# Hybrid attention/mLSTM layer: PSUM banks of the second merge, and the places and emission points of the output weights

## The chip, the cores and the metric

One core of one Trainium2 chip. The metric is the device time of one execution in microseconds (us). Before the change, three runs gave 844.54, 844.98 and 847.42 us, so the median is 844.98 us.

## The reference

One decoder layer works on `x`, 1024 tokens by 1024 features, in float32. A pre-norm and one wide projection feed two mixers, a differential attention `ya` (4 heads) and an mLSTM `yb` (4 heads). What the change touches is the end of the layer:

```
merged = sigmoid(ga) * (ya @ w_a) + sigmoid(gb) * (yb @ w_b)
out    = merged @ w_out
x      = x + rmsnorm(out, norm_post)
```

Here `ya` and `yb` are 1024 x 512, `w_a` and `w_b` 512 x 1024 and `w_out` 1024 x 1024.

## The kernel before

Every float32 matrix product is done as three products of a rounded high part and a low remainder (high x high, and the two mixed ones). `split` (line 113) makes the two parts of a tile: ScalarE (ACT) casts the high part, and VectorE (DVE) subtracts it to get the low part. So each weight tile and each intermediate tile costs one ACT and one DVE instruction before TensorE (PE) can use it.

The layer's last three stages are these.

The first merge (`merge_b`, line 1092) multiplies the mLSTM outputs by `w_b`. It is a generator, and its matmuls are pulled piece by piece between the steps of the last attention heads, so that PE has work while softmax runs on DVE and ACT. `merge` (line 1062) works through 8 column blocks `d` of 128 and two token halves, so 16 blocks of 12 matmuls. Each block accumulates in one PSUM bank, and DVE line 1083 then reads the bank and the stored gate `tg` and writes the product back into `tg`. `keep_b` stores that in DRAM (`m_d`).

The second merge does the same with the attention outputs and `w_a`. Its `finish_a` (line 1151) loads the stored first half (`mb`), adds it on DVE (line 1154) and splits the sum into high and low parts `M[kh, T, e]`: `kh` is the half of the columns, `T` the half of the tokens and `e` the high or low part. All 16 blocks take their bank from `acc`, a pool of 3. The other five banks are in the pool `misc`, used by scores, transposes and half of the output tiles.

The output stage (from line 1191) goes over the column halves `cc` and the eight token tiles `tt`. Each of the 16 groups is 24 matmuls, over `kt` from 0 to 7, with `M` as the stationary and `wide[cc, kh, k, e]`, the split output weights, as the moving operand. The order within a `kt` is M high with weight high, M high with weight low, M low with weight high. `out_weights(cc, kh)` loads one quarter of `w_out` in two pieces `g` of 512 KB through `raw_tile` (4 buffers, shared with the merges' weights and with `load_y`), and splits each piece into tiles called here the homes: for (0, 0) the tiles 21h and 21l, for (0, 1) t2h and t2l, for (1, 0) t1h and t1l, for (1, 1) three `wc` buffers and slot 12. The tiles t1 and t2 hold the attention outputs `ys_a` until the second merge's matmuls end. The tiles 21h and 21l hold two of the mLSTM outputs until the first merge ends. The residual rows `xr` take slots 8 to 11, which the last attention head uses before (slot 8: its output; 9 and 10: keys; 11: the mask).

Each engine runs its instructions in an order that is fixed when the program is built. The planner takes the emission order as priority, but lets a later instruction go ahead where it expects the engine to be free and the operands to be there. So an instruction can run well before the place where its line stands, and then holds up what is queued behind it if its data come later than planned. All transfers shown are issued from one queue, SP, in such an order.

Of the kernel before, what the change touches and what calls it, by code (L numbers as in the profile page):

```python
# [10 lines left out]
F32R = mybir.dt.float32r  # L11
# [5 lines left out]
P = 128  # L17
# [22 lines left out]
def kernel(  # L40
# [16 lines left out]
    nc = tc.nc  # L57

    cp = ctx.enter_context(tc.tile_pool(name="cp", bufs=1))
    hp = ctx.enter_context(tc.tile_pool(name="hp", bufs=1))  # L60
# [8 lines left out]
    w_a_v = w_a[0].rearrange("(k p) n -> p k n", p=P)  # L69
    w_b_v = w_b[0].rearrange("(k p) n -> p k n", p=P)  # L70
    w_out_v = w_out[0].rearrange("(k p) n -> p k n", p=P)
# [7 lines left out]
    def mm(*args, **kw):  # L79
        pin(nc.tensor.matmul(*args, **kw))  # L80
# [7 lines left out]
    def acc(name):  # L88
        return ps_acc.tile([P, 512], F32, tag="acc", name=name)
# [4 lines left out]
    def slot(i, shape, name, dtype=F32):  # L94
        return tp.tile(shape, dtype, tag=f"T{i}", name=name)

    def part(name, dtype=F32):
        return tp.tile([P, 512], dtype, tag="st", name=name, bufs=5)

    def temp(name):  # L100
        return tp.tile([P, 512], F32, tag="tm", name=name, bufs=4)

    def raw_tile(shape, name):
        return wp.tile(shape, F32, tag="raw", name=f"raw_{name}", bufs=4)

    def wc_tile(shape, name, dtype=F32R):
        return wp.tile(shape, dtype, tag="wc", name=name, bufs=3)

    def drain(gen):
        for _ in gen:  # L110
            pass

    def split(raw, hi, lo):
        nc.scalar.copy(hi, raw)  # L114
        nc.vector.tensor_sub(lo, raw, hi.bitcast(F32))
# [370 lines left out]
    def hs_(T):  # L486
        return slice(T * 512, T * 512 + 512)
# [561 lines left out]
        left[0] -= pulled[0] - was  # L1049


    def load_y(slot0, heads, tags):
        ys = []
        for h in heads:
            r = raw_tile([P, S], f"yr{slot0 + h}")
            nc.sync.dma_start(r, y_d[slot0 + h])
            t = hp.tile([P, 2, S], F32R, tag=f"h{tags[h]}", name=f"y{slot0 + h}")
            split(r, t[:, 0], t[:, 1])
            ys.append(t)
        return ys  # L1060

    def merge(name, w_v, which, ys, finish):
        for d in range(8):
            if d % 2 == 0:
                r = raw_tile([P, 4, 2, P], f"{name}{d}")
                nc.sync.dma_start(
                    r.rearrange("p k n c -> p k (n c)"), w_v[:, :, d * P : d * P + 256]
                )
            w = wc_tile([P, 2, 4, P], f"{name}w{d}")
            split(r[:, :, d % 2], w[:, 0], w[:, 1])  # L1070
            for half in range(2):
                tg = temp("tg")
                nc.sync.dma_start(tg, g_d[which * 8 + d][:, hs_(half)])
                ps = acc("mrg")
                for kt in range(4):
                    for j, (a, b) in enumerate(((0, 0), (0, 1), (1, 0))):
                        mm(
                            ps, w[:, a, kt], ys[kt][:, b, hs_(half)],
                            start=(kt == 0 and j == 0), stop=(kt == 3 and j == 2),
                        )  # L1080
                    if kt % 2:
                        yield 1.4
                nc.vector.scalar_tensor_tensor(  # L1083
                    out=tg, in0=tg, scalar=1.0, in1=ps, op0=ALU.add, op1=ALU.mult
                )
                finish(d, half, tg)
# [5 lines left out]
    ys_a = []  # L1092

    def merge_b():
        ys = load_y(4, range(4), ("11h", "11l", "21h", "21l"))
        n = 0
        for due in merge("mb", w_b_v, 1, ys, keep_b):
            yield due
            n += 1
            if n == 20:  # L1100
                ys_a.extend(load_y(0, range(3), YA))
        done.add("mb")


    PAIR, MB = 7 * 12 * 0.2325, 16 * 12 * 0.2325
    fill.append(run_pairs(pairs))
    fill.append(merge_b())
    total = len(pairs) * PAIR + MB
    weave(gate_chain())
# [35 lines left out]
    for kh in range(2):  # L1145
        for T in range(2):
            for e in range(2):
                tag = (("t3h", "t3l"), ("22h", "22l"), ("t4h", "t4l"), ("11h", "11l"))[kh * 2 + T][e]
                M[kh, T, e] = hp.tile([P, 4, 512], F32R, tag=f"h{tag}", name=f"m{kh}{T}{e}")

    def finish_a(d, half, tg):
# [2 lines left out]
        nc.vector.tensor_add(tg, tg, mb)  # L1154
        split(tg, M[d // 4, half, 0][:, d % 4], M[d // 4, half, 1][:, d % 4])

    drain(merge("ma", w_a_v, 0, ys_a, finish_a))


    npost = slot(13, [P, D], "npost")  # L1160
# [1 line left out]
    orow = [slot(i, [P, D], f"o_{i}") for i in range(8)]  # L1162
    ssq = cp.tile([P, NT, 2], F32, name="ssq")

    wide = {}

    def out_weights(cc, kh):

        if (cc, kh) == (1, 1):
            home = [  # L1170
                wc_tile([P, 2, 512], f"wo{n}") if n < 3 else slot(12, [P, 2, 512], "wo3", F32R)
                for n in range(4)
            ]
            for k in range(4):
                for e in range(2):
                    wide[cc, kh, k, e] = home[(k // 2) * 2 + e][:, k % 2]
            dst = [[home[g * 2 + e] for e in range(2)] for g in range(2)]
        else:
            names = (("21h", "21l"), ("t2h", "t2l"), ("t1h", "t1l"))[cc * 2 + kh]
            home = [hp.tile([P, 4, 512], F32R, tag=f"h{n}", name=f"wo{n}") for n in names]  # L1180
            for k in range(4):
                for e in range(2):
                    wide[cc, kh, k, e] = home[e][:, k]
            dst = [[home[e][:, g * 2 : g * 2 + 2] for e in range(2)] for g in range(2)]
        for g in range(2):
            r = raw_tile([P, 2, 512], f"o{cc}{kh}{g}")
            k0 = kh * 4 + g * 2
            nc.sync.dma_start(r, w_out_v[:, k0 : k0 + 2, cc * 512 : cc * 512 + 512])
            split(r, *dst[g])

    for cc in range(2):
        for kh in range(2):
            out_weights(cc, kh)
        c0 = cc * 512
        for tt in range(NT):
            ts_ = slice(tt * P, (tt + 1) * P)
            js = slice((tt % 4) * P, (tt % 4 + 1) * P)
            ps = (misc if tt % 2 else acc)("out")
            for kt in range(KT):
                for i, (a, b) in enumerate(((0, 0), (0, 1), (1, 0))):  # L1200
                    mm(
                        ps, M[kt // 4, tt // 4, a][:, kt % 4, js], wide[cc, kt // 4, kt % 4, b],
                        start=(kt == 0 and i == 0), stop=(kt == KT - 1 and i == 2),
                    )
            junk = part("oj")
            nc.scalar.activation(  # L1206
                junk, ps, AF.Square, scale=D ** -0.5, accum_out=ssq[:, tt, cc : cc + 1]
            )
            orr = orow[tt]
            nc.vector.tensor_mul(orr[:, c0 : c0 + 512], ps, npost[:, c0 : c0 + 512])  # L1210
            if cc == 0:
                nc.gpsimd.tensor_scalar(
                    ssq[:, tt, 0:1], ssq[:, tt, 0:1], 1.0, 4.0 * EPS, ALU.mult, ALU.add
                )
                continue
            st = sp.tile([P, 3], F32, tag="ost", name="ost")
            nc.gpsimd.tensor_add(st[:, 0:1], ssq[:, tt, 0:1], ssq[:, tt, 1:2])
            nc.gpsimd.tensor_tensor(st[:, 2:3], st[:, 0:1], mhalf[:, 0:1], ALU.pow)
            xr = slot(8 + tt % 4, [P, D], "xr")
            nc.sync.dma_start(xr, x[0, ts_, :])  # L1220
            for n0 in range(0, D, 512):
                ns = slice(n0, n0 + 512)
                nc.vector.scalar_tensor_tensor(
                    out=orr[:, ns], in0=orr[:, ns], scalar=st[:, 2:3], in1=xr[:, ns],
                    op0=ALU.mult, op1=ALU.add,
                )
                nc.sync.dma_start(out[0, ts_, ns], orr[:, ns])
# [28 lines left out]
```

## Time and profile before

| what | value |
|---|---|
| median of three runs | 844.98 us |
| the profiled execution | 845.01 us |
| its span | 843.3 us |
| PE busy | 828.1 us (98%) |
| DVE busy | 571.8 us (68%) |
| ACT busy | 401.1 us (48%) |
| POOL busy | 38.4 us (5%) |

The span is the time from the first to the last recorded instruction, and 1.71 us of the profiled execution lie outside it. Matmuls overlap one another, so a recorded matmul is longer than the distance to the next one. A stall is best read from the distance between starts. In a row of the timeline, the part in brackets says how long the engine sat idle before the instruction and what ended that.

### The profile page before, as it was taken

Reading aid. Unit: us, or ns where it says so; the run is one execution under the profiler, and the core shown is the slowest. Engines: PE = TensorE matmul, PEld = TensorE weight load, DVE = VectorE, ACT = ScalarE, POOL = GpSimd, SP = SyncE. Lnnn points to the kernel's source line nnn. Section 1 sums busy time; section 2 is a strip of 40 time slices with the busy share of each in tenths; the row PEclk is TensorE's granted clock in tenths of the full one; section 3 lists DMA queues with packets and bytes.
Section 4 is the critical chain, followed back from the end, with each engine's and each line's share of the span. In section 5 each row is a group of like instructions: output and inputs, shape, how many; then the busy total and the mean of one; then the engine's idle time right before and its main releaser. Section 6 shows DMA issues by size and latency. Waiting matters only on the chain.

```text
span 843.3 us, 12218 instructions
## 1 busy us (share of the span) xinstructions
PE 828.1 (98%) x4282; PEld 705.7 (84%) x4282; DVE 571.8 (68%) x1161; ACT 401.1 (48%) x892; POOL 38.4 (5%) x70
## 2 busy tenths in 40 slices
PE   9999999999999999999999999999999999999997
PEld 7998888888888888888888888878888887778885
DVE  6996969769659766568767865587586645881133
ACT  6654545544554544446646654466676412341110
POOL 1100000000000000020010000000100000000011
PEclk9999999999999999999999999999999999999999
DMA  7712342442552557276256336433766869840062
GB/s 246 213 38 76 94 146 59 134 158 56 170 162 75 175 157 231 84 211 200 69 184 204 126 94 206 150 137 96 226 205 225 284 195 295 274 137 1 1 199 100
DMA packets 100482, 128.44 MB, mean 152 GB/s; under 512 B 8666, under 2 KB 60098, under 8 KB 100420
## 3 DMA queue, kind: packets, MB, share of 16 engines
q1 hardware_dynamic: 100420, 127.66, 48.1%
q8 instruction: 34, 0.56, 0.3%
q14 instruction: 28, 0.23, 0.1%
HBM read 88.27 MB, written 39.35 MB: 151 GB/s over the span
## 4 chain that ended last, share of the span: by engine, by line
PE 84%; DMA 7%; DVE 4%; ACT 2%; issue 2%; SPq 1%; POOL 0%; DVEq 0%; POOLq 0%; ACTq 0%
PE out L80 10%; PE tok L80 6%; PE S L80 4%; PE pv L80 3%; DMA m_d<-tg 3%; PE mrg L80 2%; PE pT L83 2%; PE num L80 1%; DMA zs<-z_d 1%; PE qkb0Y L80 1%; PE g04Y L80 1%; PE g00Y L80 1%; PE za1Y L80 1%; PE g02Y L80 1%; PE g12Y L80 1%
## 5 line engine op out<-in xcount | busy, mean ns | idle before, releaser
L956 ACT ACTIVATE p<-p,ast 128x128 f32<-128x128 f32 (+7 forms) x64 | 49.6, 776 | 29.7 <-DVE ast L955 21.6
L949 DVE CUSTOM_DVE_ANT_0 p<-S,gm 128x384 f32<-128x384 f32 (+5 forms) x96 | 49.9, 554 | 18.2 <-PE S L80 16.5
L1210 DVE TENSOR_TENSOR o<-out,npost 128x512 f32<-128x512 f32 x16 | 11.1, 691 | 57.0 <-ACT oj L1206 57.0
L80 PE MATMUL mrg<-y,maw 128*128 128x512 f32 x192 | 44.0, 390 | 1.8 <-DVE tg L1083 1.8
L80 PE MATMUL mrg<-y,mbw 128*128 128x512 f32 x192 | 44.9, 391 | 0.0
L80 PEld LDWEIGHTS mrg<-y,maw 128*128 128x128 f32 x192 | 36.0, 188 | 9.7 <-DVE tg L1083 2.2
L1206 ACT ACTIVATE oj<-out 128x512 f32<-128x512 f32 x16 | 9.6, 598 | 69.2 <-PE out L80 69.1
L80 PEld LDWEIGHTS mrg<-y,mbw 128*128 128x128 f32 x192 | 35.8, 188 | 7.3
L80 PEld LDWEIGHTS pv<-va,pT 128*128 128x128 f32 x288 | 37.2, 191 | 2.7
L80 PE MATMUL pv<-va,pT 128*128 128x128 f32 x288 | 37.4, 275 | 0.0
L80 PE MATMUL S<-khh,qs 128*128 128x384 f32 (+5 forms) x96 | 34.7, 367 | 0.0
L80 PE MATMUL S<-kll,qs 128*128 128x384 f32 (+5 forms) x96 | 32.4, 342 | 0.4 <-DMA kll<-qk_d 0.4
L1083 DVE SCALAR_TENSOR_TENSOR tg<-tg,mrg 128x512 f32<-128x512 f32 x32 | 21.8, 682 | 16.0 <-PE mrg L80 13.1
L754 DVE SCALAR_TENSOR_TENSOR cv<-pad,cols,cv 128x1024 f32<-128x1024 f32 x24 | 30.7, 1279 | 0.2
L970 DVE SCALAR_TENSOR_TENSOR p<-p,ast,p 128x128 f32<-128x128 f32 (+7 forms) x32 | 26.1, 816 | 0.7
L823 ACT ACTIVATE junk<-raw 128x128 bf16<-128x128 f32 x32 | 9.9, 310 | 32.3 <-DVE raw L818 32.1
L83 PE MATMUL pT<-ident,p 128*128 128x128 f32 x144 | 21.2, 274 | 3.5 <-DVE p L970 3.4
L995 ACT ACTIVATE oa<-pv 128x128 f32<-128x128 f32 x32 | 8.9, 277 | 30.9 <-PE pv L80 30.8
L986 ACT COPY pT<-pT 128x512 f32<-128x512 f32 (+3 forms) x48 | 21.7, 488 | 3.3 <-PE pT L83 3.2
L80 PE MATMUL out<-wo,m 128*128 128x512 f32 x96 | 23.1, 389 | 0.0
L114 ACT CAST m<-tg 128x512 fp32r<-128x512 f32 x16 | 9.9, 621 | 24.4 <-DVE tg L1154 24.4
L80 PEld LDWEIGHTS out<-wo,m 128*128 128x128 f32 x96 | 18.0, 188 | 3.7
(1240 smaller groups left out, 2474.9 us busy)
## 6 DMA issues: line engine op xcount, KB each, us to landing
raw_g<-in_w_in_dram SPq DMA_DIRECT2D x16, 512.0 KB, 4.1
g_d<-g SPq DMA_DIRECT2D x32, 256.0 KB, 3.8
tg<-g_d SPq DMA_DIRECT2D x32, 256.0 KB, 3.8
raw_qkb<-in_w_in_dram SPq DMA_DIRECT2D x16, 256.0 KB, 3.1
z_d<-zt SPq DMA_DIRECT2D x16, 256.0 KB, 3.1
zs<-z_d SPq DMA_DIRECT2D x16, 256.0 KB, 5.2
raw_qka<-in_w_in_dram SPq DMA_DIRECT2D x16, 256.0 KB, 3.1
qk_d<-qah SPq DMA_DIRECT2D x16, 256.0 KB, 2.1
```

Source lines behind the costliest of these rows:

```text
L80: pin(nc.tensor.matmul(*args, **kw))
L83: pin(nc.tensor.transpose(out=out, in_=in_, identity=ident))
L114: nc.scalar.copy(hi, raw)
L754: nc.vector.scalar_tensor_tensor(out=cv, in0=pad[:, t : t + S], scalar=cols[:, t * 8 + blk : t * 8 + blk + 1], in1=cv, op0=ALU.mult, op1=A ...
L823: nc.scalar.activation(junk, raw[:, c, 0:P], AF.Square, accum_out=stbs[h, c // 4][:, 1, c % 4 : c % 4 + 1])
L949: nc.vector.tensor_tensor_reduce(out=pr[:, n0:n1], in0=pss[:, : n1 - n0], in1=gm[:, (7 - i) * P + n0 : (7 - i) * P + n1], scale=-0.125, sc ...
L956: nc.scalar.activation(pr[:, :nk], pr[:, :nk], AF.Exp, bias=nm, scale=-1.0, accum_out=sth[:, c, i : i + 1],)
L970: nc.vector.scalar_tensor_tensor(out=p0[:, :nk], in0=p1[:, :nk], scalar=st[:, 3:4], in1=p0[:, :nk], op0=ALU.mult, op1=ALU.add,)
L986: nc.scalar.copy(pT[:, j0:j1], pt[:, 0 : (j1 - j0) * P].rearrange("p (j t) -> p j t", t=P))
L1083: nc.vector.scalar_tensor_tensor(out=tg, in0=tg, scalar=1.0, in1=ps, op0=ALU.add, op1=ALU.mult)
L1206: nc.scalar.activation(junk, ps, AF.Square, scale=D ** -0.5, accum_out=ssq[:, tt, cc : cc + 1])
L1210: nc.vector.tensor_mul(orr[:, c0 : c0 + 512], ps, npost[:, c0 : c0 + 512])
```

## The change

The second merge takes its banks in turn from `acc` and `misc`. The first quarter of the output weights, (0, 0), gets the tiles t4h and t4l as homes, and its two pieces are emitted inside the first merge, after its 8th and its 14th yield of 32. The second quarter, (0, 1), gets slots 8 to 11. The quarters (1, 0) and (1, 1) get t2 and t1. `M[1, 0]` moves from t4h and t4l to 21h and 21l. The quarters other than (0, 0) are emitted where they were. The `wc` buffers and slot 12 no longer hold output weights.

```diff
+    def out_weights(cc, kh, g):
+        if (cc, kh) not in homes:
+            tags = {(0, 0): ("t4h", "t4l"), (1, 0): ("t2h", "t2l"), (1, 1): ("t1h", "t1l")}
+            if (cc, kh) in tags:
+                two = [
+                    hp.tile([P, 4, 512], F32R, tag=f"h{t}", name=f"wo{t}") for t in tags[cc, kh]
+                ]
+                homes[cc, kh] = [[two[e][:, n * 2 : n * 2 + 2] for e in range(2)] for n in range(2)]
+            else:
+                four = [slot(8 + n, [P, 2, 512], f"wo{n}", F32R) for n in range(4)]
+                homes[cc, kh] = [four[0:2], four[2:4]]
...
+        r = raw_tile([P, 2, 512], f"o{cc}{kh}{g}")
+        k0 = kh * 4 + g * 2
+        nc.sync.dma_start(r, w_out_v[:, k0 : k0 + 2, cc * 512 : cc * 512 + 512])
+        split(r, *dst)
...
-    def merge(name, w_v, which, ys, finish):
+    def merge(name, w_v, which, ys, finish, banks=None):
+        banks = banks or (acc,)
...
-                ps = acc("mrg")
+                ps = banks[(d * 2 + half) % len(banks)]("mrg")
...
             n += 1
+            if n in (8, 14):
+                out_weights(0, 0, (n - 8) // 6)
...
-                tag = (("t3h", "t3l"), ("22h", "22l"), ("t4h", "t4l"), ("11h", "11l"))[kh * 2 + T][e]
+                tag = (("t3h", "t3l"), ("22h", "22l"), ("21h", "21l"), ("11h", "11l"))[kh * 2 + T][e]
...
-    drain(merge("ma", w_a_v, 0, ys_a, finish_a))
+    drain(merge("ma", w_a_v, 0, ys_a, finish_a, (acc, misc)))
...
         for kh in range(2):
-            out_weights(cc, kh)
+            for g in range(2):
+                if (cc, kh) != (0, 0):
+                    out_weights(cc, kh, g)
```

## Rows read from the trace of the kernel before

**Rows 1.** Page, part 1: busy us, share of the span, instructions.
```profile
PE 828.1 (98%) x4282; PEld 705.7 (84%) x4282; DVE 571.8 (68%) x1161; ACT 401.1 (48%) x892; POOL 38.4 (5%) x70
```

**Rows 2.** Waits of PE, whole span: us in total, times, longest.
```profile
PE pT L83 <- DVE p L970: 3.4, 3, 1.5
PE mrg L80 <- DVE tg L1083: 1.8, 1, 1.8
PE out L80 <- DVE wot2l L115: 1.8, 2, 1.3
```

**Rows 3.** Timeline of PE, second merge into output stage: start, us, instruction, idle before.
```profile
701.95 13.76 PE L80 MATMUL mrg<-y,maw 128*128 128x512 f32 x60
717.52 30.22 PE L80 MATMUL mrg<-y,maw 128*128 128x512 f32 x132 [1.81 <-DVE tg L1083]
747.57 0.39 PE L80 MATMUL out<-wo21h,m 128*128 128x512 f32 x1
...
754.10 0.50 PE L80 MATMUL out<-wot2l,m 128*128 128x512 f32 x1 [1.28 <-DVE wot2l L115]
...
755.36 0.39 PE L80 MATMUL out<-wo21h,m 128*128 128x512 f32 x1
```

**Rows 4.** Timeline of ACT: the first read of two successive output groups.
```profile
761.02 0.60 ACT L1206 ACTIVATE oj<-out 128x512 f32<-128x512 f32 x1 [2.54 <-PE out L80]
766.46 0.60 ACT L1206 ACTIVATE oj<-out 128x512 f32<-128x512 f32 x1 [4.75 <-PE out L80]
```

**Rows 5.** Timeline of DVE in the second merge and at its end.
```profile
706.22 0.69 DVE L1083 SCALAR_TENSOR_TENSOR tg<-tg,mrg 128x512 f32<-128x512 f32 x1 [2.69 <-DMA tg<-g_d]
...
715.04 1.22 DVE L115 TENSOR_TENSOR wo21l<-raw_o,wo21h 128x1024 fp32r<-128x1024 f32 x1 [4.15 <-ACT wo21h L114]
...
716.79 0.68 DVE L1083 SCALAR_TENSOR_TENSOR tg<-tg,mrg 128x512 f32<-128x512 f32 x1
...
748.57 0.68 DVE L1083 SCALAR_TENSOR_TENSOR tg<-tg,mrg 128x512 f32<-128x512 f32 x1
...
749.89 1.22 DVE L115 TENSOR_TENSOR wot2l<-raw_o,wot2h 128x1024 fp32r<-128x1024 f32 x1
751.03 0.68 DVE L1083 SCALAR_TENSOR_TENSOR tg<-tg,mrg 128x512 f32<-128x512 f32 x1
751.62 0.68 DVE L115 TENSOR_TENSOR m<-tg,m 128x512 fp32r<-128x512 f32 x1
```

**Rows 6.** Timeline of ACT in the second merge and at its end.
```profile
713.96 1.05 ACT L114 CAST wo21h<-raw_o 128x1024 fp32r<-128x1024 f32 x1 [5.15 <-DMA raw_o<-in_w_out_dram]
...
750.01 0.62 ACT L114 CAST m<-tg 128x512 fp32r<-128x512 f32 x1 [0.18 <-DVE tg L1154]
750.53 1.99 ACT L114 CAST wot1h<-raw_o 128x1024 fp32r<-128x1024 f32 x2
```

**Rows 7.** Timeline of the SP queue: one residual load, the first output weights.
```profile
694.24 0.38 SPq L1220 DMA_DIRECT2D xr<-in_x_dram  x1
...
707.83 0.39 SPq L1188 DMA_DIRECT2D raw_o<-in_w_out_dram  x1
```

**Rows 8.** Windows, two merge stages: length, engines' busy us, PEclk, DMA share, GB/s.
```profile
645.80:702.00 56.20, 56.20 (x291) 48.05 (x291) 29.95 (x60) 18.07 (x39) 1.64 (x1) 1.00 0.78 251
702.00:747.50 45.50, 43.69 (x193) 35.87 (x192) 32.87 (x50) 13.41 (x22) 0.00 (x0) 1.00 0.78 261
```

**Rows 9.** Timelines of DVE and PE: last two attention tiles, combined and transposed.
```profile
657.29 1.15 DVE L970 SCALAR_TENSOR_TENSOR p<-p,ast,p 128x896 f32<-128x896 f32 x1
...
667.66 1.28 DVE L970 SCALAR_TENSOR_TENSOR p<-p,ast,p 128x1024 f32<-128x1024 f32 x1
...
660.13 0.93 PE L83 MATMUL pT<-ident,p 128*128 128x128 f32 x7
...
672.50 1.04 PE L83 MATMUL pT<-ident,p 128*128 128x128 f32 x8
```

**Rows 10.** Tile view of the residual rows: time from issue to landing.
```profile
DMA to landing us min/median/max: 3.5/4.1/4.7
```

More of the change, by code (lines that the diff above doesn't have):

```diff
@@ L1049, in until @@
         left[0] -= pulled[0] - was
+    wide, homes = {}, {}
+    def out_weights(cc, kh, g):
[9 more added lines that the diff above has]
+                homes[cc, kh] = [four[0:2], four[2:4]]
+        dst = homes[cc, kh][g]
+        for k in range(2):
+            for e in range(2):
+                wide[cc, kh, g * 2 + k, e] = dst[e][:, k]
+        r = raw_tile([P, 2, 512], f"o{cc}{kh}{g}")
+        k0 = kh * 4 + g * 2
+        nc.sync.dma_start(r, w_out_v[:, k0 : k0 + 2, cc * 512 : cc * 512 + 512])
+        split(r, *dst)
     def load_y(slot0, heads, tags):
@@ L1163 @@
     ssq = cp.tile([P, NT, 2], F32, name="ssq")
[L1165 to L1189, printed above, removed]
     for cc in range(2):
         for kh in range(2):
-            out_weights(cc, kh)
+            for g in range(2):
+                if (cc, kh) != (0, 0):
+                    out_weights(cc, kh, g)
         c0 = cc * 512
```

## The prediction

> **What bounds the kernel now.** I read the engine totals first, then the waits of TensorE (PE), then the timelines of the engines around each wait that the diff can reach. The totals show PE busy for 828.1 of 843.3 us [rows 1]. There is no second resource to trade against: the change can only gain where PE stands still, and it can lose anywhere.
>
> The list of PE's waits has two entries in the stages that the diff touches [rows 2]: 1.8 us in the merge, on VectorE's (DVE) line 1083, and 1.8 us in the output stage, on the low parts of the weights `wot2l`. The wait lists hide part of a stall under the modelled tail of the matmul before, so I size both by the distances between starts [rows 3].
> - Merge: 132 matmuls run from 717.52 to 747.57, 0.2277 us each. The first 60 should have taken 13.66 us and end at 715.61, but the next starts at 717.52. The stall is 1.91 us.
> - Output: successive groups of 24 matmuls are 766.46 - 761.02 = 5.44 us apart when nothing waits [rows 4], 0.2267 us each. The first group takes from 747.57 to 755.36, 7.79 us. The stall is 2.35 us.
>
> Together that is 4.26 us, 0.50% of the time, and the ceiling of what the change can win there. A measurement of this kernel tells about 0.3%, 2.5 us, from no change.
>
> Why does each occur? In the merge, five blocks (60 matmuls) run, and the sixth needs the bank of the third, because the pool holds three. DVE reads the third block's bank only at 716.79, since it stood idle 4.15 us for the cast of an output-weight piece and then spent 1.22 us on it [rows 5]. The cast itself waited 5.15 us for that piece to land [rows 6], which was issued at 707.83 [rows 7]. In the output stage the home of quarter (0, 1) is the tile pair t2, which the merge's own matmuls read to the end, so its splits can only start when PE is already there.
>
> **The change part by part.**
>
> Eight banks in the second merge. Even blocks rotate over three banks and odd blocks over five, so block b needs the bank of block b-6 or b-10. With PE going on at 0.2277 us a matmul from 701.95, the seventh block starts at about 718.3 and needs the bank that DVE read at 706.22 [rows 5]. From 716.79 to 748.57 DVE reads twelve more, one in 2.65 us, so no block waits for a bank. The stall of 1.91 us goes; its other end would be 0, if something else stopped PE at the same place, and the nearest is the weight split of column block 4, which PE would want at 723.8. I take the whole: -1.91, and the second merge then ends at 747.57 - 1.91 = 745.66.
>
> Quarter (0, 1) in slots 8 to 11. These are free once the last head is transposed: before, the last residual load, which takes slot 8, issues at 694.24 [rows 7]. Its raw buffers are those that quarter (0, 0) had, freed by the merge's own weight splits, so I expect its pieces where those of (0, 0) were, from about 707.8, with the same DVE work (two splits of 1.22 us). They would be done long before PE needs them. The 2.35 us go: -2.35; were the pieces loaded as late as now, 0 (a rival below).
>
> What is late next. With both stalls gone PE starts the output at 745.66 and wants the 24th matmul of the first group, which reads the low part of the last `M` tile of the first token half, at 745.66 + 23 x 0.2267 = 750.87. Before, DVE finishes that tile at 751.62 + 0.68 = 752.30 [rows 5]; PE stalled longer on the weights, so nobody saw it. DVE reads the 15th block's bank at 748.57, 3.7 us after PE ended it, and it is behind because of the wait at 715, not because of PE. A faster PE does not move it. So the question is what DVE has in front of that split. Before there is one `wot2l` split (749.89). If it stays, as a split of quarter (1, 0) in the same home and freed by the same matmuls, PE waits 752.30 - 750.87 = 1.43 us. If it goes, the split moves up 1.14 us but must follow the cast that ends at 750.63 [rows 6], so it ends near 751.32, and PE waits 0.45 us. Is it likely to stay? ACT ran both `wot1h` casts, emitted after the whole first column half, at 750.53, ahead of the last `M` cast [rows 6]. Low priority therefore does not keep weights out of that place, and I take +1.43.
>
> Here a rule stands against the row. "Perfetto Trace Analysis" in the Trainium skill, section Optimizing Tensor Performance, says that independent accumulation groups should rotate through different banks so that evacuating one overlaps the next group's matmuls; taken alone it promises the whole 4.26 us. "PSUM — Partial Sum Buffer" in the Trainium skill, section Engine vs sequencer instructions, says that VectorE's queue is strictly first in, first out; by that rule the banks only move the queue's lateness to the first reader of `M`, and 4.26 - 1.43 remains. The trace agrees with the second: the bank read at 716.79 stood behind the weight split at 715.04 [rows 5].
>
> Quarter (0, 0) inside the first merge. It adds two loads of 512 KB, two casts of 1.05 us and two splits of 1.22 us to a stage where DVE is busy 29.95 and ACT 18.07 of 56.20 us [rows 8]. DMA is busy to 0.78 there, but the change also takes four residual loads of 512 KB out of it (slots 8 to 11 are no longer free), so traffic falls. In the second merge as many pieces can load as before. Cost taken: 0, hidden under PE's matmuls. The other end is in the slower rival: DVE held while attention needs it. The two raw buffers are also taken from the `load_y` pieces and the merges' later weights, which load ahead of their use; I take 0 for that too.
>
> Residual rows later. They now wait for quarter (0, 1)'s last reader, the end of the first column half. The first is wanted after the next group and its norm, 5.44 us or more later, and a load lands in 3.5 to 4.7 us [rows 10]. Cost 0; at worst, with the load issued only at the end of the half and 0.45 us of issue, still within 5.44 us. `M[1, 0]` in 21h and 21l: free when the first merge ends at 701.95, written only from the second merge's ninth block, which PE starts at 723.8: 0.
>
> Sum: -1.91 - 2.35 + 1.43 = -2.83 us on the profiled 845.01, 842.18. The profiled execution is 0.03 us from the median, so the forecast for the median is 842.2.
>
> **The rivals.**
>
> *The lateness of DVE is gone too.* If the planner orders DVE's tail without the weight split, the sum is -4.26 + 0.45, 841.2; if the hold at 715 shrinks as well (694's residual load no longer delays the stores that the gate loads wait for), the full 4.26 come: 840.8. For it: the quarters in t2 and t1 have become low priority. Against: the casts at 750.53.
>
> *DVE later than before.* If both splits of the t2 home get ahead of that `M` split, it is finished 1.14 us later still, at 753.44; PE waits 2.57 and the time is 843.3. If quarter (0, 1) is loaded only after the merge, the 2.35 stay and the time is 843.1: the part of the change that it then does not do. If the hold at 715 is longer, every microsecond of it reaches PE through `M`: 3 us more give 845.2.
>
> *Slower: quarter (0, 0) holds DVE in the attention tail.* PE transposes the last two attention tiles at 660.13 and 672.50, and DVE has them combined at 658.44 and 668.94, so the slack is 1.69 and 3.56 us [rows 9]. A piece whose data come late holds DVE as at 715, 4.15 + 1.22 = 5.37 us [rows 5]. One hold in front of each tile costs 3.68 + 1.81 = 5.49 us, against 2.83 gained: 847.7. It decides from a loss of 2.83 us, and shows as slower by more than 0.3% above 5.4. For it: PE already waits three times for such tiles, 3.4 us in all [rows 2]. Against: DVE and ACT are little used there and traffic falls [rows 8].
>
> **How the numbers follow.** Forecast 0.42, with its own range 841.5 to 843.0; DVE's lateness gone too 0.27; DVE later than before 0.18; slower 0.13. Below 842.45 it counts as faster: six tenths of the forecast (0.25) and all of the first rival make 0.52. Above 847.5 it is slower: 0.13. The rest, 0.35, is the same. The range of 840.5 to 846.5 leaves out half of a tenth below and the slower rival above.
>
> **What would show it right or wrong.** PE's waits should have no entry for line 1083 in the merge and none for weights in the output stage, and one new entry of 0.4 to 1.5 us, output on `m`. PE should run the 192 matmuls of the second merge in 43.7 us. DVE's split of the 15th `M` tile should end 750 to 752.5 us into the span. The prediction is wrong if PE stalls between 645 and 702, or if DVE's tail is more than 2 us later than now.

## The result

The kernel after took 842.30 us (median of 14 runs, 840.57 to 845.30) beside 847.05 us for the kernel before on the same chip (14 runs, 844.54 to 849.04). The ratio is 0.9948, with a 95% interval of 0.9934 to 0.9961: faster by 0.5%. The forecast was 842.2 us. The time came out, the gain did not: 2.83 us were forecast from the 844.98 us of three runs, and 4.75 us were measured from the 847.05 us of fourteen. A base that was 2.07 us too low and a gain that was 1.92 us too small nearly cancel. Of the terms of the sum two came out, one did not, and two costs were not foreseen.

First the page of the kernel after, part 1, which answers to [rows 1]: busy us, share, instructions.

```profile
PE 829.3 (99%) x4282; PEld 706.5 (84%) x4282; DVE 573.0 (68%) x1161; ACT 400.4 (48%) x892; POOL 36.5 (4%) x70
```

Then the list of PE's waits over the whole span, which answers to [rows 2]: us in total, times, longest.

```profile
PE pT L83 <- DVE p L970: 2.5, 2, 1.5
PE warm L169 <- DVE mprev L699: 1.1, 1, 1.1
PE xT L83 <- DVE x L223: 0.4, 1, 0.4
PE S L80 <- DMA kll<-qk_d: 0.4, 1, 0.4
PE S L80 <- ACT pT L986: 0.2, 1, 0.2
```

Both entries of the last stages are gone, `mrg` on `tg` and `out` on `wot2l`. No entry for `out` on `m` has come, which the prediction expected. New is `S` on ACT's `pT`, 0.23 us at 662.34. A stall of PE between 645 and 702 was one of the two signs that the prediction named as showing it wrong; this one is small, and the first row of the table below shows 0.66 us lost in that stretch. The timeline of PE from the second merge on, against [rows 3] (start, us, instruction):

```profile
702.57 43.68 PE L80 MATMUL mrg<-y,maw 128*128 128x512 f32 x192
746.09 0.39 PE L80 MATMUL out<-wot4h,m 128*128 128x512 f32 x1
...
751.61 0.39 PE L80 MATMUL out<-wot4h,m 128*128 128x512 f32 x1
...
757.17 0.39 PE L80 MATMUL out<-wot4h,m 128*128 128x512 f32 x1
...
762.71 0.39 PE L80 MATMUL out<-wot4h,m 128*128 128x512 f32 x1
```

All 192 matmuls of the merge stand in one row, without a pause. The output groups start 5.52, 5.56 and 5.54 us apart; before they were 5.44 us apart when nothing waited [rows 4]. So the two profiles differ as follows. The stretches go from start to start of matmuls; groups 2 to 16 end with the last matmul, at 837.14 and 834.07.

| stretch | before, us | after, us | difference | predicted |
|---|---|---|---|---|
| first matmul of the first merge to that of the second | 56.11 | 56.77 | +0.66 | 0 |
| second merge | 45.62 | 43.52 | -2.10 | -1.91 |
| first output group | 7.79 | 5.52 | -2.27 | -2.35 + 1.43 |
| output groups 2 to 16 | 81.78 | 82.46 | +0.68 | 0 |

These sum to -3.03 us; the spans differ by 3.1 us (843.3 and 840.2). By the medians it is 4.75 us. The totals of single profiles are a coarse measure: the first matmul of the first merge alone stands anywhere from 644.38 to 647.77 us in the fourteen profiles of this study (645.84 in before, 645.80 in after).

Why did PE not wait for `M`? The timeline of DVE in the kernel after, against [rows 5]:

```profile
705.78 0.69 DVE L1108 SCALAR_TENSOR_TENSOR tg<-tg,mrg 128x512 f32<-128x512 f32 x1 [1.19 <-DMA tg<-g_d]
706.50 0.69 DVE L1181 TENSOR_TENSOR tg<-tg,mb 128x512 f32<-128x512 f32 x1
711.85 1.23 DVE L115 TENSOR_TENSOR wo<-raw_o,wo 128x1024 fp32r<-128x1024 f32 x1 [4.66 <-ACT wo L114]
713.00 0.69 DVE L115 TENSOR_TENSOR m<-tg,m 128x512 fp32r<-128x512 f32 x1
713.60 0.68 DVE L1108 SCALAR_TENSOR_TENSOR tg<-tg,mrg 128x512 f32<-128x512 f32 x1
...
748.79 1.22 DVE L115 TENSOR_TENSOR wot2l<-raw_o,wot2h 128x1024 fp32r<-128x1024 f32 x1
749.92 0.68 DVE L1108 SCALAR_TENSOR_TENSOR tg<-tg,mrg 128x512 f32<-128x512 f32 x1
750.52 0.68 DVE L115 TENSOR_TENSOR m<-tg,m 128x512 fp32r<-128x512 f32 x1
```

The hold is still there (4.66 us idle for the cast of an output-weight piece), but the split stands 9.28 us after the merge's first matmul; before it stood 715.04 - 701.95 = 13.09 us after it [rows 3, 5], and behind one more bank read in DVE's order. The `wot2l` split did stay ahead of the `m` split, as predicted. The 15th `M` tile is ready at 750.52 + 0.68 = 751.20, and the matmul that reads its low part starts at 751.38. It is 0.18 us early.

### The profile page after: what moved, and what is told of

It reads as the page before. It is cut to its first block, busy times and chain, and to the rows that moved or that the text cites. A ratio compares the mean times of both kernels' runs of the same rounds, so it can differ in the third digit from the quotient of the medians.

```text
span 840.2 us, 12224 instructions
## 1 busy us (share of the span) xinstructions
PE 829.3 (99%) x4282; PEld 706.5 (84%) x4282; DVE 573.0 (68%) x1161; ACT 400.4 (48%) x892; POOL 36.5 (4%) x70
## 4 chain that ended last, share of the span: by engine, by line
PE 95%; DMA 2%; DVE 1%; ACT 1%; issue 1%; SPq 0%; POOL 0%; DVEq 0%; POOLq 0%; ACTq 0%
PE out L80 10%; PE mrg L80 10%; PE tok L80 6%; PE S L80 4%; PE pv L80 4%; PE pT L83 2%; PE num L80 2%; PE qkb0Y L80 1%; PE g04Y L80 1%; PE g00Y L80 1%; PE za1Y L80 1%; PE g12Y L80 1%; PE g02Y L80 1%; PE zb0Y L80 1%; PE za0Y L80 1%; PE g10Y L80 1%
## 5 line engine op out<-in xcount | busy, mean ns | idle before, releaser
L970 DVE SCALAR_TENSOR_TENSOR p<-p,ast,p 128x128 f32<-128x128 f32 (+7 forms) x32 | 26.1, 816 | 0.7
L995 ACT ACTIVATE oa<-pv 128x128 f32<-128x128 f32 x32 | 8.8, 276 | 26.3 <-PE pv L80 26.1
L80 PE MATMUL out<-wot4h,m 128*128 128x512 f32 x64 | 21.1, 390 | 0.0
```

Source lines behind the costliest of these rows:

```text
L970: nc.vector.scalar_tensor_tensor(out=p0[:, :nk], in0=p1[:, :nk], scalar=st[:, 3:4], in1=p0[:, :nk], op0=ALU.mult, op1=ALU.add,)
L995: nc.scalar.activation(raw[:, i], pv[:, 0:P], AF.Square, accum_out=sth[:, 2, i : i + 1])
```

## The experiments

In what follows "the hold" is DVE's idle time before the first output-weight split of the second merge, and its place is counted from that merge's first matmul to the split. The ratios are to the kernel before, measured beside each.

**The banks alone.** The kernel before with the `banks` argument of `merge`, and nothing else.

```diff
-    drain(merge("ma", w_a_v, 0, ys_a, finish_a))
+    drain(merge("ma", w_a_v, 0, ys_a, finish_a, (acc, misc)))
```

> The kernel before with one part of the change: the second merge takes its banks in turn from both pools, and all weight homes and emission points stay as before. Theory (a bank only moves VectorE's lateness to the next reader): the merge stall of 1.9 us goes, but the low weights in t2 come no earlier, since VectorE's order and its hold are the same; PE waits at the output stage some 1.9 us longer, about 4.2 instead of 2.35 us, and the time is that of before, within 0.5 us. Rival (each stall is worth its length): 1.9 us faster than before, the output stall stays at 2.35.

847.12 us, ratio 1.0004 (0.9991 to 1.0017): no gain. The merge shrank to 44.48 us, and the output stage gave more than that back. The timeline of PE:

```profile
700.68 22.37 PE L80 MATMUL mrg<-y,maw 128*128 128x512 f32 x98
723.72 21.60 PE L80 MATMUL mrg<-y,maw 128*128 128x512 f32 x94 [0.66 <-DVE maw L115]
...
749.36 0.50 PE L80 MATMUL out<-wot2h,m 128*128 128x512 f32 x1 [1.32 <-ACT wot2h L114]
751.60 0.50 PE L80 MATMUL out<-wot2l,m 128*128 128x512 f32 x1 [1.74 <-DVE wot2l L115]
754.54 0.79 PE L80 MATMUL out<-wot2l,m 128*128 128x512 f32 x1 [1.03 <-DVE wot2l L115]
```

The wait of 0.66 us is for a merge weight, whose split stands in DVE's queue behind the late hold. It is the stop that the prediction named as the nearest one behind the bank, the weight of column block 4, wanted at 723.8. The last matmul takes 0.79 us where its neighbours take 0.50, and the windows say why (us of the stretch, busy us of PE, PEld, DVE, ACT and POOL, granted clock, DMA share, GB/s):

```profile
749.00:752.00 3.00, 0.90 (x3) 0.55 (x4) 2.97 (x5) 2.81 (x5) 0.00 (x0) 1.00 0.00 0
752.00:754.00 2.00, 1.51 (x6) 0.69 (x4) 2.00 (x4) 1.58 (x3) 0.00 (x0) 0.71 0.66 209
754.00:756.00 2.00, 1.46 (x4) 1.17 (x5) 2.00 (x3) 1.03 (x1) 0.00 (x0) 0.50 0.32 99
756.00:758.00 2.00, 2.00 (x6) 1.61 (x5) 2.00 (x3) 0.87 (x4) 0.15 (x1) 0.50 0.57 216
```

After two waits close together TensorE ran at the lower of its two levels, 1.2 GHz, for some 7 us. The first output group took 11.68 us and the second 6.80, where 5.44 is the undisturbed length; that is 6.24 us in the first group, where 4.2 had been expected.

**The change without the banks.** The kernel after with the argument `(acc, misc)` taken out; the order of instructions on every engine is the same.

> The changed kernel with three banks again in the second merge; every engine's order of instructions is that of the changed kernel. Theory: with VectorE's hold where it is in the changed kernel (the third block's bank read at 715.4 instead of 716.8) PE stalls in the merge by 0 to 1.9 us at the sixth or seventh block, the first output group then waits for nothing, and the time is 0 to 1.8 us above the changed kernel, still 2 to 3 us below before. Rival (each stall is worth its length): 1.9 us above the changed kernel, with the merge stall at 1.9.

842.94 us, ratio 0.9964 (0.9945 to 0.9983). The second merge took 44.35 us, with one stall of 0.39 us listed for the bank, and the output stage waited for nothing. So with the rest of the change in place the banks are worth 0.83 us of the merge, and the change without them keeps most of the gain. The 1.91 us of the prediction's first term are what three banks cost when the hold is late.

**No early emission.** The kernel after with quarter (0, 0) emitted at the output stage like the others.

```diff
-            if n in (8, 14):
-                out_weights(0, 0, (n - 8) // 6)
```

> The changed kernel, but with the first quarter of the output weights emitted where it was before, at the output stage (its home stays t4): all four splits of the first column half's weights then fall into the second merge. Theory (VectorE's queue ends the stage): two more splits of 1.22 us in VectorE's queue make the 15th M tile some 2.4 us later than in the changed kernel, PE waits about 2.4 us for it in the first output group, and the attention tail gets back its 0.6 us; in sum 1.5 to 2 us slower than the changed kernel. Rival (only the homes count, since both quarters have free homes before the merge ends): the same as the changed kernel or 0.6 us faster.

840.48 us, ratio 0.9930 (0.9913 to 0.9947). My theory failed: it forecast a loss and the kernel is the faster one, by 1.8 us in the medians and by 0.18% in the ratios, though the two intervals still overlap. The second merge started 56.11 us after the first (56.77 in after), and the two additional splits of 1.22 us in DVE's queue delayed the 15th `M` tile by 0.4 us only (49.05 us after the merge's start, 48.63 in after), or by 1.3 us if the hold, 0.9 us earlier here, is counted in. PE waits for it, but only some 0.4 us: the first output group takes 5.91 us, 5.52 in after. DVE was idle 0.69 us, waiting for ACT's cast, before six of the 16 `m` splits in after and before four here; a split that is added there can use up such gaps first.

**Slots at low addresses.** The kernel after with the pool of the slots (`tp`) opened ahead of the pool of the split halves (`hp`); only addresses change.

> The changed kernel with the pool of the slots placed ahead of the other two in SBUF. Every engine's order of instructions is unchanged; only addresses move: slots 8 to 11 from 209,760 to 226,176 bytes per partition down to 65,888 to 82,304, with the same remainders by 64 and 128 bytes; the merges' weight and raw buffers come on top. In the changed kernel the groups of the first column half are 5.53 us apart and those of the second 5.44. Theory (the moving operand is read more slowly from the top of the partition): 5.44 us in both halves, 0.7 us faster. Rival (alignment of slot 8, which is not a multiple of 64, or the size of the tiles): 5.53 stays, same time.

841.24 us, ratio 0.9939 (0.9920 to 0.9957). The output groups of the first column half stand 5.49 us apart (5.53 in after). From start to start, the 12 matmuls on `wot4` in each, of which the first three had taken 231 to 233 ns, take 226 or 227 each; the 12 on slots 8 to 11 still take 226 to 236 (229 to 238 in after). The same matmul takes the same time in all these groups and in every profile of one placement, within 1 or 2 ns, and another time when the pool is moved (the first two groups aside). So the longer distances follow the placement of the tiles, not the schedule. The three slow ones on `wot4` go with what ran before them: the first group, behind the merge, does not have them, and the ninth group of after, whose weights lie in t2, has them (231 to 233) behind the last group on the slots. The size of the tiles alone is not it either: the quarter (1, 1) of before lay in tiles of the same size, slot 12 among them, and its matmuls took 226 to 228. What in the placement does it stays open; distances of 228 to 236 ns also stand behind the two waits in the first profile of before, with the weights in the split halves.

**Residual rows late, and nothing else.** All kernels with the early hold have one thing in common: slots 8 to 11 are taken, so that no residual row is loaded in the merge stage. Here the kernel before gets only that.

```diff
-            xr = slot(8 + tt % 4, [P, D], "xr")
+            xr = raw_tile([P, D], f"x{tt}")
```

> The kernel before, with one thing changed: the eight residual loads take the raw buffers of the weights instead of slots 8 to 11, so that none can be issued in the merge. Theory (the four early residual loads make the hold of VectorE in the second merge late; in every kernel without them it ends near 8.3 to 9.3 us after the merge's first matmul, before 13.1): here the first low split of an output weight starts 8 to 10 us after the merge's start, the merge loses at most 0.8 us although it has three banks, and the 15th M tile is ready 48 to 49.5 us after the merge's start (before 50.35). The stall on the weights in t2 stays, 2.0 to 3.5 us. Time 845 to 846, against 847 before. Rival (the new home of the weights or the early piece moved the hold): the low split still starts at 12.5 to 14 us, the stall of 1.9 us stays, and the time is that of before within 0.5 us.

842.79 us, ratio 0.9945 (0.9927 to 0.9963). One line, with no bank, no home and no emission changed, gives as much as the whole change, and 2 to 3 us more than my theory said. The hold stood at 8.99 us and the `raw_o` load was issued 2.57 us after the merge's start (before 5.88 [rows 3, 7]). The timeline of PE:

```profile
701.72 11.04 PE L80 MATMUL mrg<-y,maw 128*128 128x512 f32 x48
713.28 5.71 PE L80 MATMUL mrg<-y,maw 128*128 128x512 f32 x24 [0.52 <-DVE tg L1083]
719.34 27.47 PE L80 MATMUL mrg<-y,maw 128*128 128x512 f32 x120 [0.35 <-DVE tg L1083]
```

The stall of 1.91 us has become two short ones (the merge takes 44.92 us), and the first output group still waits, 6.96 us long. From the second merge's start to the last matmul it is 133.65 us, against 135.2 in the first profile of before and 131.5 in after.

**Late emission.** The kernel after with (0, 0) emitted after the 22nd and 26th step instead of the 8th and 14th.

> The kernel after, with quarter (0, 0) emitted after the 22nd and 26th step of the first merge instead of the 8th and 14th. Theory (its two raw buffers keep the y pieces of the merge from loading early, the casts that wait for them hold ScalarE, and the score matmuls wait for ScalarE's copies of pT): emitted later, the y pieces load early again and the distance from the first merge's first matmul to the second merge's is 56.1 us (after 56.77, before 56.11); from the second merge to the last output matmul 131.5 as in after. Time 0.6 us below after: 841 to 842. Rival (any piece of (0, 0) in the first merge costs the same, wherever it is emitted, since ScalarE and VectorE are given the same work): 56.8 us, and the time of after.

841.49 us, ratio 0.9932 (0.9914 to 0.9951). The distance between the merges is 56.11 us, as expected: the 0.66 us came from the place of the emission. The profiled execution was the slowest of the six (845.19); 2 us of that lie ahead of the merges, since its first merge starts at 647.77 (645.80 in after). Another 2 us are in the output stage: there the `raw_o` load took until 10.16 us to reach its cast, the hold stood at 11.25, and PE waited for the last `M` tile after all. The timeline of PE:

```profile
750.12 2.26 PE L80 MATMUL out<-wo,m 128*128 128x512 f32 x9
752.89 0.72 PE L80 MATMUL out<-wo,m 128*128 128x512 f32 x2 [0.52 <-ACT m L114]
754.58 0.50 PE L80 MATMUL out<-wo,m 128*128 128x512 f32 x1 [0.96 <-DVE m L115]
```

That is the term of +1.43 us of the prediction, in two parts, first for the high and then for the low part of the tile: 1.48 us in the list, and 1.99 by the distance between starts (the group takes 7.52 us, the later ones 5.53). The hold stands only 2 us later than in after. The wait is real, and the place of the hold decides over it.

**No early emission, slots low.** Both edits together.

> The kernel after with quarter (0, 0) emitted at the output stage, and the pool of the slots placed at the start of the scratch memory, ahead of the split halves. Theory (both observations add: 0.65 us in the attention tail, and 0.04 us in each of eight output groups): 0.3 to 0.5 us below the kernel without early emission alone, 840.0 to 840.4, a span of 838.0 to 838.6, output groups of the first half 5.49 us apart. Rival (the address has nothing to do with the slower groups): 5.53 us and 840.5.

840.53 us, ratio 0.9927 (0.9909 to 0.9945). The groups stand 5.49 us apart, but the time is that of the kernel without early emission alone (840.48); 0.3 us can't be told apart here. These two are the fastest kernels of the study by their medians; their intervals overlap with that of after (0.9934 to 0.9961).

**The kernel before, again.** One profile, no edit.

> The kernel before, unchanged, for a second profile: its profiled execution of 845.0 lies 1.6 to 2 us below the medians of 846.6 to 847.1. Theory (the gain by medians, 4.4 us, is more than the 3.1 us between the two profiles because the output stage of before has more than one course, in which TensorE's granted clock falls after its waits, as in the kernel with the banks alone, where it was 0.58 for 5 us): this profile shows an output stage that ends 136 to 139 us after the second merge's start (135.2 in the first profile), with a granted clock below 1 between 750 and 763. Rival (the difference lies upstream, in the mLSTM or the attention stages): 135.2 us again, and the second merge starts after 702.5.

The theory was right on the clock and wrong on the place: it fell in the merge, not in the output stage. The timeline of PE, and the windows around the pause:

```profile
702.83 13.76 PE L80 MATMUL mrg<-y,maw 128*128 128x512 f32 x60
719.42 33.04 PE L80 MATMUL mrg<-y,maw 128*128 128x512 f32 x132 [2.83 <-DVE tg L1083]
```

```profile
702.00:716.40 14.40, 14.40 (x65) 11.74 (x63) 5.83 (x9) 2.31 (x4) 0.00 (x0) 1.00 0.84 281
716.40:719.40 3.00, 0.19 (x1) 0.00 (x0) 2.43 (x4) 1.02 (x2) 0.00 (x0) 0.87 0.87 270
719.40:722.00 2.60, 2.58 (x6) 2.10 (x7) 1.29 (x2) 0.89 (x1) 0.00 (x0) 0.50 0.94 332
722.00:725.00 3.00, 3.00 (x8) 2.32 (x8) 2.81 (x4) 1.54 (x4) 0.00 (x0) 0.50 0.60 188
725.00:728.00 3.00, 3.00 (x13) 2.42 (x13) 3.00 (x6) 1.42 (x3) 0.00 (x0) 0.93 0.93 339
```

The hold stood at 14.11 us and the stall was 2.93 us long, 1 us more than in the first profile. After it the granted clock was 0.50 until about 725, and the 132 matmuls that had taken 30.05 us took 32.87. The stall thus cost the merge 2.93 + 2.82 us. Part of that came back: PE reached the weights in t2 later, and the first output group took 5.65 us, 7.79 in the first profile. From the second merge's start to the last matmul it was 136.9 us beside 135.2, which is 1.7 of the 2.6 us between the two profiles. Another 1.0 us lies ahead of it (57.13 us between the merges, 56.11 in the first profile), where PE waited 0.70 us for a bank of the first merge. This execution took 847.57 us, near the median of 847.0; the first profile, 845.01, is one of the shorter executions. "TensorE: Matmul & The Clock Gate" in the Trainium skill, section HAM oscillation, says that a wait for data can send the array back to the half rate, so that the next matmuls start slow. The trace agrees, with 0.50 behind this stall; behind the stall of 1.91 us in the first profile the clock stayed at 1.00.

**Four extra loads in the kernel after.** Residual rows that nothing reads, into slots that come free in the first merge.

```diff
+    for n, i in enumerate((4, 5, 2, 6)):
+        xe = slot(i, [P, D], "xe")
+        nc.sync.dma_start(xe, x[0, n * P : n * P + P, :])
```

> The kernel after, with four more loads of residual rows (512 KB each) into slots 4, 5, 2 and 6, where nothing reads them; they are issued when those slots come free, in the first merge, as the four residual loads of before were. Theory (such loads, in SP's queue and on the DMA engines, make the merge's own transfers late, and with them the first piece of output weights and VectorE's hold): the first output-weight load of the second merge is issued 4 to 7 us after that merge's start (after 2.39, before 5.88), the first low split starts 11 to 14 us after it (after 9.28, before 13.09); TensorE does not stall in the merge, because it has eight banks, but the 15th M tile is ready at 50 to 52 us (after 48.63) and the output stage waits for it 1 to 3 us. Time 843.5 to 845. Rival (the loads are harmless where the weights have homes of their own): 9.3 us, and the time of after within 0.5 us, 842 to 842.8.

843.66 us, ratio 0.9963 (0.9949 to 0.9976): 1.4 us slower than after by the medians, with overlapping intervals, inside the expected range, but not by the expected way. They were issued at 668.25 to 684.39, the `raw_o` load 1.96 us after the merge's start, and the hold stood at 8.66 us, where it was. The loss in this profile lies in the attention tail, before the first of these loads; up to there the order on every engine is that of the kernel after. The timelines of PE and ACT:

```profile
664.04 0.50 PE L80 MATMUL S<-khh,qs 128*128 128x512 f32 x1 [2.63 <-ACT pT L986]
```

```profile
662.20 1.04 ACT L114 CAST y<-raw_yr 128x1024 fp32r<-128x1024 f32 x1 [5.75 <-DMA raw_yr<-y_d]
663.15 0.27 ACT L995 ACTIVATE oa<-pv 128x128 f32<-128x128 f32 x1
```

This is the cost of the early emission at its worst. Its two pieces take two raw buffers, the loads of `y` pieces of the merge wait until their splits have freed them, ACT waits for a piece in its fixed order, and the copies of the attention tile stand behind the cast. The same row of the kernel after, and from SP's list of waits there (640 to 660 us; us in total, times, longest) the wait for the buffers:

```profile
660.50 1.05 ACT L114 CAST y<-raw_yr 128x1024 fp32r<-128x1024 f32 x1 [3.30 <-DMA raw_yr<-y_d]
```

```profile
SPq L1080 <- DVE wot4l L115: 2.7, 2, 1.3
```

The five profiles with the early emission have 56.75, 56.77, 56.83, 57.35 and 59.21 us between the merges, the three with (0, 0) emitted late or at the output stage 56.11, 56.11 and 56.17. The four loads did not set SP's queue back further in this profile: counted from the first merge's first matmul it was 2.4 us behind that of after just ahead of them, and 2.0 us at the `raw_o` load. What the 1.4 us of the medians are made of was not shown.

**Residual rows late, with the banks.** Both edits on the kernel before.

> The kernel before with the residual loads in the raw buffers, as in the run with late residual loads, and the second merge over all eight banks. Theory (the banks only hand VectorE's lateness on, to the weights in t2 and the last M tile): the second merge takes 43.5 to 43.8 us (44.92 with three banks), the first output group takes 7.5 to 9 us (6.96), and the time is within 0.5 us of the run without the banks: 842.3 to 843.3. Rival (with the hold early the banks win what the merge still loses, 1.3 us, since the first group's wait is bounded by the weights that are there): 841.2 to 841.8.

842.62 us, ratio 0.9950 (0.9933 to 0.9966), the time without the banks. The merge fell to 43.52 us and the first output group grew to 8.48. The timeline of PE has the weights in t2, still read by the merge to its end, in the bank's place:

```profile
701.71 43.68 PE L80 MATMUL mrg<-y,maw 128*128 128x512 f32 x192
...
749.48 0.50 PE L80 MATMUL out<-wot2l,m 128*128 128x512 f32 x1 [1.15 <-DVE wot2l L115]
752.42 0.50 PE L80 MATMUL out<-wot2l,m 128*128 128x512 f32 x1 [1.28 <-DVE wot2l L115]
```

**The kernel after, again.** One profile, no edit.

> The kernel after, unchanged, for a second profile. Theory (its gain by medians is more than the 3.1 us between the first two profiles, because before has executions in which TensorE's granted clock falls behind its stall in the merge, as the second profile of before shows, 0.72 from 716 to 728; a kernel without a stall there has none): granted clock of 1.00 from 702 to 763, the second merge in 43.4 to 43.8 us, 131.2 to 132 us from its start to the last output matmul. Rival (after has such executions too): a granted clock below 0.95 somewhere between 702 and 763, and 133 us or more.

841.76 us, and as the theory said: clock 1.00 from 702 to 763, a merge of 43.52 us, 131.47 us from its start to the last matmul.

**One residual load late.** Only slot 8's residual loads, the one at 694.24 among them, go through the raw buffers.

```diff
-            xr = slot(8 + tt % 4, [P, D], "xr")
+            xr = slot(8 + tt % 4, [P, D], "xr") if tt % 4 else raw_tile([P, D], f"x{tt}")
```

> The kernel before, in which only the residual loads of slot 8 (the one issued at 694.24, and its second use) go through the raw buffers; the three loads issued at 662 to 667 stay. Theory (it is the order of SP's queue and of VectorE's that the load at 694 changes: behind it the mb loads, and with them the first output-weight piece and its split, come one gate load and one block later; the traffic of the other three does not matter): the first output-weight load is issued 2 to 3 us after the second merge's start (before 5.88, with all residual loads late 2.57), the first low split starts 8.5 to 9.5 us after it (13.09, 8.99), and the time is that of the kernel with all residual loads late, 842.3 to 843.3. Rival (traffic of 512 KB loads in the first merge makes the merge's transfers late): the split starts at 10.5 to 13.5 us, and the time is 844.5 to 847.

845.23 us, ratio 0.9977 (0.9963 to 0.9991): the rival's numbers, so my theory fell. SP's queue took the order of the kernel with all residual loads late around the weights, as the theory said, and the first `raw_o` load was issued 3.81 us after the merge's start; but its cast began at 10.40 us (7.91 there) and the split stood at 11.48. The timeline of PE:

```profile
702.86 11.04 PE L80 MATMUL mrg<-y,maw 128*128 128x512 f32 x48
716.91 34.33 PE L80 MATMUL mrg<-y,maw 128*128 128x512 f32 x144 [3.00 <-DVE tg L1083]
```

With the split one block earlier in DVE's order, three banks stop PE one block earlier, after 48 matmuls, and a piece that lands late costs 3.00 us. Here too the granted clock fell, to 0.50 until about 720:

```profile
717.00:718.00 1.00, 1.00 (x3) 0.81 (x4) 1.00 (x3) 0.00 (x0) 0.00 (x0) 0.50 0.86 334
```

So the order is one part of what the residual loads did, and not the whole. The traces show some of the rest. A gate load (`tg`) waits until an earlier store `m_d` has landed (27.1 us in all in SP's queue from 660 to 707), so a queue that has fallen behind can pass that on from load to load. The timelines of SP in this kernel, and in the one with all residual loads late:

```profile
666.49 0.38 SPq L1220 DMA_DIRECT2D xr<-in_x_dram  x1
...
671.93 0.32 SPq L1073 DMA_DIRECT2D tg<-g_d  x1
...
706.67 0.39 SPq L1188 DMA_DIRECT2D raw_o<-in_w_out_dram  x1
```

```profile
668.61 0.32 SPq L1073 DMA_DIRECT2D tg<-g_d  x1
...
704.29 0.41 SPq L1188 DMA_DIRECT2D raw_o<-in_w_out_dram  x1
```

Counted from the first merge's first matmul, the gate load behind the three residual loads comes after 26.1 us here, after 23.2 in the other kernel and 24.4 in that with the banks as well; the `raw_o` load after 60.9, 58.9 and 58.5. In the first profile of before, though, the gate load behind the same three comes after 24.4 us, no later than there, and the queue falls back only behind the load at 694.24: the first `mb` load after 52.4 us, 49.3 and 49.4 there. So the theory fits that execution and not this one. What decides whether the three loads set the queue back, and why the piece here took 6.59 us from issue to cast (5.34 with all residual loads late), stays open.

## Why the prediction was right, step by step

**What bounds the kernel: right.** The gain lies where PE stood still in the merge and the first output group, and the list of waits showed both.

**Eight banks, -1.91: the size was right, the cause only half.** After has no stall in the merge. But the banks alone gained nothing (1.0004) and with the residual loads late nothing again (842.62 beside 842.79), and the change without them lost 0.83 us of the merge. The prediction named DVE's queue as the place the lateness would go to; that is what both runs show, only that the first to be late for PE were the weights in t2, not `M`.

**Quarter (0, 1) in slots 8 to 11, -2.35: right.** With the `out` on `m` wait at zero, the first group is 2.27 us shorter. From the kernel with late residual rows and banks to the one without early emission, a step that changes little but the homes, the group falls from 8.48 to 5.91 us and the median from 842.62 to 840.48; by the ratios (0.9950 and 0.9930) that is 1.7 us, with overlapping intervals.

**The 15th `M` tile, +1.43: the step that failed.** The sentence "A faster PE does not move it" is true (the tile is ready 48.83 and 48.92 us after the merge's start in the two kernels with late residual rows, whose merges take 44.92 and 43.52 us); the hold that sets DVE's lateness moved, from 13.09 to 9.28 us. I took the hold as given because the same piece would be loaded through the same buffers, and expected its loads "where those of (0, 0) were, from about 707.8". They came at 704.96, with the residual loads gone from the merge stage, which in the kernel before is enough to bring them forward. The prediction had this in the first rival, in parentheses, for the load at 694 alone, and gave the time 840.8 for it. That this edit of the change, which it costed at 0 as "residual rows later", would by itself bring the kernel before to 842.79 us it did not see.

**Quarter (0, 0) early, 0: mis-sized.** It cost 0.66 us in the profile, and 0.6 to 3.1 over five profiles, against the 56.11 us of the kernels without it. (The second profile of before, and that with one residual load late, have 57.13 and 57.04 us there, from a wait for a bank of the first merge.) The mechanism is near the slower rival's (a piece that comes late holds an engine in the attention tail), but the engine is ACT, the late piece is a `y` of the merge, and the price is that of one short wait. The clause that took 0 for the raw buffers taken from `load_y` is where it went wrong.

**Not foreseen: +0.68 us** for matmuls whose moving operand lies in slots 8 to 11, 0.09 us in each of eight groups, the three slow matmuls behind each of them included.

So the profile's sum of -3.03 beside a forecast of -2.83 is partly luck: a wait of 1.43 that did not come stands against 1.34 of costs that were not foreseen. Luck, too, is the time itself, since the error of the base hid that of the gain. The rest of the gain by medians, 4.75 us beside 3.1, fits executions of the kernel before that lose clock behind the stall, as its second profile does, but that was not shown: of 65 runs of it 24 have a mean granted clock of 0.994 or less over the span, of 60 runs of after and all its variants 5 have. That mean is a coarse sign: of the 12 runs with one residual load late none has it, though their profile shows the clock at 0.50 behind the stall. How much each run lost there was not measured, and in that second profile 1.0 of the 2.6 us lie ahead of the second merge.

## What to carry to other kernels

When an engine with a fixed order idles for a transfer, ask first what stands in front of that transfer in its queue and who else moves data then: here four prefetches of rows that were wanted 100 us later cost 4 us, and one line that delays them was worth as much as new banks, homes and emission points together. Not every such load does that: four others of that size, spread over the same stage of the kernel after, did not set the queue back further in the one profile there is. More PSUM banks do not speed up their reader; price them at nothing until the next consumer of that reader's results has slack. And a home that is free early can still be the dearer one: look at what the early tenant keeps out (buffers, in this case) and at the start-to-start time of the matmuls that read it.

## What the runs showed of the hardware

- Behind a pause of 2.93 us in the merge TensorE's granted clock was 0.50 (1.2 GHz) for some 6 us and added 2.82 us (second profile of before); behind one listed at 3.00 us it was 0.50 for some 3 us and added 1.4 us (one residual load late). Behind one of 1.91 us it stayed at 1.00 (first profile of before).
- Matmuls of one shape (128x512 moving, float32 parts) differed by their operands' placement: mostly 226 or 227 ns from start to start with the weights in the split halves and nothing waited for, 226 to 238 with them in slots 8 to 11, constant to 2 ns for each matmul of a group and changed by moving the pool.
- A DVE split of 1.22 us put into a queue with idle gaps of 0.69 us cost less than its length: two of them (2.44 us) delayed the end of the queue by 0.4 to 1.3 us.
